# Seven block products for eight in the gate and up projections of a macaron layer

## The chip, the cores and the metric

The kernel runs on one core of a Trainium2 chip. The metric is the device time of one execution in microseconds (us). The core has a matrix engine (TensorE, PE in the profile, with its weight loads as PEld), a vector engine (DVE), a scalar engine (ACT), GpSimd (POOL) and a queue engine (SP) that issues most DMAs.

## The reference

One encoder layer on 256 tokens of width 2048, all in float32; the feed-forward width is 5632:

```python
def swiglu(h, w_gate, w_up, w_down):
    return (jax.nn.silu(h @ w_gate) * (h @ w_up)) @ w_down

x = x + 0.5 * swiglu(rms_norm(x, ffn1_norm), ffn1_w_gate, ffn1_w_up, ffn1_w_down)
# [u | q | k | v] = rms_norm(x) @ w_in; diagonal SSM on u, stick-breaking attention on q, k, v;
# x = x + concat(rms_norm(y_ssm), rms_norm(y_sb)) @ w_out
x = x + 0.5 * swiglu(rms_norm(x, ffn2_norm), ffn2_w_gate, ffn2_w_up, ffn2_w_down)
# x = x + rms_norm((p @ w_ple_proj) * sigmoid(rms_norm(x) @ w_ple_gate))
```

The change lies in `h @ w_gate` and `h @ w_up` of both feed-forward networks.

## The kernel before

**Tiling.** Tokens stand in two row tiles of 128 (`TT` = 2, index t). The contraction over 2048 has 16 k tiles of 128 (`KD`), and they are handled in quarters of four. Columns go in blocks of 512 (`NB`), so gate and up have 11 column blocks (`NF`), index f. Each FFN runs over f: `gemm_block` for the gate's block, SiLU on ACT out of PSUM (L410), `gemm_block` for up's block, then a multiplication on DVE into `hh` (L430), which `turned` transposes (two DVE transposes, L203, and DMAs into `hT`). After the 11 blocks comes the down projection, whose left side is split from `hT` by `act`.

**Three passes.** A float32 product is made of three matmuls in a rounded format: each operand is split into a high part (a cast on ACT, L168) and the remainder (a subtraction on DVE, L171); the passes are high x high, low x high and high x low. `gemm_half` (L284, L285, L289) does this for two k tiles and both row tiles: 12 matmuls of 128x128 by 128x512. The left side (the normed tokens, tiles `nhi`/`nlo` or `hhi`/`hlo`) is split once an FFN; the weights are split as they come.

**Buffers.** A quarter of k of a column block (1 MiB) is loaded by one DMA on SP's queue into `raw` (three buffers), and split into two halves of `whi`/`wlo` (four buffers each). Four PSUM accumulators (`acc`) of 512 columns take the results. `halves("n")` has four buffers of hi and lo, `halves("h")` two. In FFN 1 the left side stands in the four n buffers, and the h buffers are used from the down projection on; in FFN 2 the left side takes both h buffers and two of the n buffers.

**Order.** The program is written in one order; a scheduler then lays out each engine's queue by simulated readiness, with the written order as priority, except where `pin` holds it. `put_off(n, fn)` calls fn after n further calls of `step()`, which stands after each half. In FFN 1, the first blocks also carry side work (`s5_prep`), which is over at f = 6.

Of the kernel before, what the change touches and what calls it, by code (L numbers as in the profile page):

```python
# [9 lines left out]
F32 = mybir.dt.float32  # L10
F32R = mybir.dt.float32r
I32 = mybir.dt.int32
AF = mybir.ActivationFunctionType
ALU = mybir.AluOpType
AX = mybir.AxisListType

P = 128
# [9 lines left out]
NB = 512  # L27
# [6 lines left out]
def layer_kernel(ctx: ExitStack, tc: tile.TileContext, a: dict, shapes: dict, out: bass.AP):  # L34
    nc = tc.nc
    _, T, D = shapes["x"]
# [7 lines left out]
    TT = T // P  # L44
    ND = D // NB
    KD = D // P
    NF = F // NB
# [6 lines left out]
    wp = ctx.enter_context(tc.tile_pool(name="wts", bufs=4))  # L54
    actp = ctx.enter_context(tc.tile_pool(name="act", bufs=1))
# [8 lines left out]
    def uid(s):  # L64
        count[0] += 1
        return f"{s}_{count[0]}"

    def get(pool, tag, width=1024, bufs=1):
        return pool.tile([P, width], F32, tag=tag, name=uid(tag), bufs=bufs)

    def com(tag):
        return get(comp, tag, *{"sg": (1024, 1), "h": (1024, 2), "sq": (NB, 1), "mid": (2048, 1)}[tag])

    def phase(name):
        return tc.tile_pool(name=name, bufs=1, reuse_waits="tile")
# [4 lines left out]
    def acc(s="acc"):  # L80
        return accp.tile([P, NB], F32, tag="acc", name=uid(s))

    def small(n=8):
        return smp.tile([P, 8], F32, tag="sm", name=uid("sm"))[:, :n]
# [11 lines left out]
    def start(g):  # L96
        beside.append(g)
        return g

    def step():  # L100
        for g in list(beside):
            if next(g, beside) is beside:
                beside.remove(g)

    def finish(g):
        for _ in g:
            pass

    def put_off(steps, fn, *args):


        def g():
            for _ in range(steps):
                yield
            fn(*args)

        return start(g())

    def pin(ins):
        return tc.keep_in_program_order(ins)  # L120
# [44 lines left out]
    def split(hi, lo, src, scale=None, pinned=False):  # L165

        if scale is None:
            copy = nc.scalar.copy(hi, src)  # L168
            if pinned:
                pin(copy)  # L170
            nc.vector.tensor_tensor(out=lo, in0=src, in1=hi.bitcast(F32), op=ALU.subtract)  # L171
        else:
            split_each(hi.unsqueeze(1), lo.unsqueeze(1), src.unsqueeze(1), [scale])
# [96 lines left out]
    def weight_halves(w, k0, nk, n0, own=None):  # L270

        raw = wp.tile([P, 4, NB], F32, tag="raw", name=uid("raw"), bufs=3)
        src = w[k0 * P : (k0 + nk) * P, n0 : n0 + NB].rearrange("(j p) n -> p j n", p=P)
        nc.sync.dma_start(raw[:, :nk, :], src)
        return weight_split(raw, nk, own)

    def gemm_half(ps, half, ts, start, stop, cols=slice(0, NB)):

        (ahi, alo), (h, hi, lo) = half
        for j in range(2):  # L280
            for t in ts:
                lh = ahi[:, 2 * h + j, t * P : (t + 1) * P]
                ll = alo[:, 2 * h + j, t * P : (t + 1) * P]
                nc.tensor.matmul(ps[t], lhsT=lh, rhs=hi[:, j, cols], start=start and j == 0, stop=False)  # L284
                nc.tensor.matmul(ps[t], lhsT=ll, rhs=hi[:, j, cols], start=False, stop=False)  # L285
        for j in range(2):
            for t in ts:
                lh = ahi[:, 2 * h + j, t * P : (t + 1) * P]
                nc.tensor.matmul(ps[t], lhsT=lh, rhs=lo[:, j, cols], start=False, stop=stop and j == 1)  # L289

    def gemm_block(act, w, n0, nkt, first=()):

        ps = [acc(), acc()]
        for k0 in range(0, nkt, 4):
            part = act(k0 // 4)
            quarter = first[k0 // 4] if k0 // 4 < len(first) else weight_halves(w, k0, min(4, nkt - k0), n0)
            for half in list(quarter):
                k = k0 + 2 * half[0]
                gemm_half(ps, (part, half), range(TT), k == 0, k + 2 == nkt)
                if first and half[0] == 0 and k0 + 4 < nkt:  # L300
                    act(k0 // 4 + 1)
                step()
        return ps
# [75 lines left out]
    def ffn(i, xn, nxt, bg=None):  # L379
        wg, wu, wd = (a[f"ffn{i}_w_{s}"][0] for s in ("gate", "up", "down"))  # L380
        hT = []
        pools = ExitStack()
        early = 6 if bg else NF
        hp = pools.enter_context(phase(f"h{i}"))
        side = ExitStack()
        prep = bg(side) if bg else None
        mids = {}

        def turned(hp, f, hh):
            pair, n_pair = f // 2, min(2, NF - f // 2 * 2) * 4  # L390
            if f % 2 == 0:
                mids[pair] = com("mid")[:, : 128 * TT * n_pair].rearrange(
                    "p (q t b f) -> p q t b f", q=4, t=TT, b=32
                )
            for t in range(TT):
                turn_blocks(mids[pair], hh[:, t * NB : (t + 1) * NB], t, f % 2 * 4, 4)
            if f % 2 or f == NF - 1:
                hf = get(hp, f"hT{pair}", T * n_pair)
                turn_quarters(hf.rearrange("p (t s f) -> p t s f", t=TT, f=n_pair), mids[pair], 8)
                hT.append(hf.rearrange("p (s f) -> p f s", f=n_pair))  # L400

        for f in range(NF):
            if prep and f == min(early, NF - 1):
                finish(prep)
                side.close()
                prep = None
                hp = pools.enter_context(phase(f"h{i}b"))
            def gate():
                for t in range(TT):
                    nc.scalar.activation(sg[:, t * NB : (t + 1) * NB], pg[t], AF.Silu, scale=xn.rs(t))  # L410

            first = ()
            if f == 0 and bg:
                warm_up(10)
                first = first_quarters(wg, xn)
            pg = gemm_block(xn, wg, f * NB, KD, first)
            sg = com("sg")
            if f == 0 and bg:
                for n in range(ND):
                    put_off(n, load_x, n)  # L420
                    put_off(n + 2, xn.squares, n)
                put_off(6, gate)
            else:
                gate()
            pu = gemm_block(xn, wu, f * NB, KD)
            if prep and f == 0:
                start(prep)
            hh = com("h")
            for t in range(TT):
                nc.vector.scalar_tensor_tensor(  # L430
                    out=hh[:, t * NB : (t + 1) * NB], in0=pu[t], scalar=xn.rs(t),
                    in1=sg[:, t * NB : (t + 1) * NB], op0=ALU.mult, op1=ALU.mult,
                )
            put_off(2, turned, hp, f, hh)

        def act(k):
            hi, lo = halves("h")
            split(hi, lo, hT[k // 2][:, k % 2 * 4 : k % 2 * 4 + 4, :])
            return hi, lo

        for n in range(ND):
            ps = gemm_block(act, wd, n * NB, F // P)
            for t in range(TT):
                nc.vector.scalar_tensor_tensor(
                    out=xt[t][n], in0=ps[t], scalar=0.5, in1=xt[t][n], op0=ALU.mult, op1=ALU.add
                )
            put_off(2, nxt.block, n)
        pools.close()
# [575 lines left out]
    q0, k0, v0 = SW, SW + NH * DH, SW + 2 * NH * DH  # L1024
    mix, s5p, atp = ExitStack(), ExitStack(), ExitStack()
    mixp = mix.enter_context(phase("mix"))
    pool = s5p.enter_context(phase("s5"))
# [10 lines left out]
    pool = atp.enter_context(phase("attn"))  # L1038
# [7 lines left out]
    for n in range(2):  # L1046
        ps = gemm_block(nm, w_in, v0 + n * NB, KD)
# [6 lines left out]
    for n, side in ((0, 0), (1, 0), (0, 1), (1, 1), (2, 0), (2, 1), (3, 0), (3, 1)):  # L1054
        y, r = ((yss, rss), (ysb, rsb))[side]
        ps = gemm_block(lambda k: y[k], w_out[side * SW : (side + 1) * SW, :], n * NB, SW // P)
        for t in range(TT):
            nc.vector.scalar_tensor_tensor(
                out=xt[t][n], in0=ps[t], scalar=r[0][:, t : t + 1], in1=xt[t][n], op0=ALU.mult, op1=ALU.add
# [30 lines left out]
    for n in range(ND - 1):  # L1090
        ps = gemm_block(npl, a["w_ple_gate"][0], n * NB, KD)
        gate = com("sg"), com("h")
        for t in range(TT):
            sigmoid(gate[0], t, ps[t])
        ps = gemm_block(lambda k: pT, a["w_ple_proj"][0], n * NB, PD // P)
        for t in range(TT):
            ple(n, t, gate, ps[t])
    n = ND - 1
    gate = com("sg"), com("h")
# [8 lines left out]
    t = 0  # L1108
    sigmoid(gate[0], t, next(gates))
    ple(n, t, gate, next(projs))  # L1110
    s = small(1)
    nc.vector.tensor_reduce(out=s, in_=ss[t], axis=AX.X, op=ALU.add)
    r = rsqrt_mean(s, D, 1)
# [4 lines left out]
    t = 1  # L1118
# [3 lines left out]
    sums, part, ms, root, r, tmp = (small(ND if i == 0 else 1) for i in range(6))  # L1122
    last = small(1)
    nc.vector.tensor_copy(sums[:, : ND - 1], ss[t][:, : ND - 1])
    cols = [slice(t * NB + c * W, t * NB + (c + 1) * W) for c in range(2)]
# [10 lines left out]
    def scaled(c):  # L1136
# [15 lines left out]
        both, lhsT=diag, rhs=es[by_pe][:, t * NB : (t + 1) * NB], start=False, stop=True, skip_group_check=True  # L1152
# [75 lines left out]
```

## Time and profile before

| what | value |
|---|---|
| runs, median of 3 (lowest, highest) | 1901.69 us (1900.64, 1903.12) |
| profiled execution, first to last instruction | 1898.3 us |
| TensorE busy | 1888.4 us, 9142 matmuls |
| DVE busy | 1299.6 us |
| ACT busy | 1105.7 us |
| POOL busy | 30.6 us |
| moved by DMA | 402.55 MB, 212 GB/s mean |

The profile is of one execution. Busy times are sums over the instructions of an engine; matmuls are pipelined, so that their durations (0.39 us each) overlap and the distance between the starts of two is the better measure. A group's row has the line, the engine, the operation, what it writes and reads with its shape, the count, then busy time and mean ns, then the idle time of the engine just before it and who ended that. Rows of waits give total us, times and the longest. Windows give for each engine the busy us in the stretch.

### The profile page before, as it was taken

The numbers are of one execution on the slowest core, as the hardware profiler recorded it, in microseconds if no ns is written. First come the engines' busy times: TensorE is split into PE (matmuls) and PEld (weight loads), VectorE is DVE, ScalarE is ACT, GpSimd is POOL, SyncE is SP. The second block draws the span as 40 slices with busy tenths as digits, with TensorE's granted clock in tenths as the row PEclk, the third lists the DMA queues.
The fourth block names the chain that finished last, engine by engine and source line by source line (L and its number), as shares of the span: only waits on it lengthen the run. The fifth ranks groups of instructions, "written<-read, shape, count | busy, mean of one in ns | idle before, by whom it ended". The sixth has DMA issues, their size and how long they took to land.

```text
span 1898.3 us, 23928 instructions
## 1 busy us (share of the span) xinstructions
PE 1888.4 (99%) x9142; PEld 1563.8 (82%) x9142; DVE 1299.6 (68%) x1604; ACT 1105.7 (58%) x1217; POOL 30.6 (2%) x48
## 2 busy tenths in 40 slices
PE   9999999999999999999999999999999999999998
PEld 7888888888888888888898888888888888888886
DVE  8996765555688987686567655555555568898855
ACT  7466664444578886455785544444444457888754
POOL 0000000000000000010010000000000000000000
PEclk9999999999999999999999999999999999999999
DMA  8677877666656657776545656665656665666553
GB/s 323 225 243 260 261 247 236 197 209 209 215 185 209 209 190 277 235 243 205 172 156 172 222 187 217 200 210 191 220 189 216 201 223 188 205 209 209 196 200 122
DMA packets 225714, 402.55 MB, mean 212 GB/s; under 512 B 16704, under 2 KB 46656, under 8 KB 225472
## 3 DMA queue, kind: packets, MB, share of 16 engines
q1 hardware_dynamic: 212976, 385.99, 61.2%
q10 hardware_dynamic: 12624, 15.04, 2.3%
q8 instruction: 71, 1.16, 0.3%
q14 instruction: 43, 0.35, 0.1%
HBM read 369.53 MB, written 14.68 MB: 202 GB/s over the span
## 4 chain that ended last, share of the span: by engine, by line
PE 94%; DVE 2%; ACT 1%; issue 1%; DMA 1%; SPq 0%; DVEq 0%; ACTq 0%
PE acc L284 30%; PE acc L285 30%; PE acc L289 30%; DVE hlo L171 1%; ACT hhi L168 1%; DVE wlo L171 1%; DVE nlo L180 1%; PE aux L715 0%; PE acc L994 0%; PE acc L989 0%; PE acc L985 0%; PE aux L634 0%; DMA raw<-in_ffn_w_gate 0%; DMA h<-in_p_turned 0%; PE aux L767 0%
## 5 line engine op out<-in xcount | busy, mean ns | idle before, releaser
L171 DVE TENSOR_TENSOR wlo<-raw,whi 128x1024 fp32r<-128x1024 f32 x666 | 810.5, 1225 | 451.5 <-ACT whi L168 446.9
L168 ACT CAST whi<-raw 128x1024 fp32r<-128x1024 f32 x666 | 697.8, 1054 | 710.1 <-PE acc L285 658.4
L284 PE MATMUL acc<-whi,nhi 128*128 128x512 f32 x1568 | 614.2, 392 | 1.2 <-ACT whi L252 0.7
L285 PE MATMUL acc<-whi,nlo 128*128 128x512 f32 x1568 | 610.6, 389 | 0.0
L289 PE MATMUL acc<-wlo,nhi 128*128 128x512 f32 x1568 | 420.7, 389 | 0.0
L285 PE MATMUL acc<-whi,hlo 128*128 128x512 f32 x1056 | 411.6, 390 | 0.7
L284 PE MATMUL acc<-whi,hhi 128*128 128x512 f32 x1056 | 411.0, 389 | 0.0
L284 PEld LDWEIGHTS acc<-whi,nhi 128*128 128x128 f32 x1568 | 294.3, 188 | 64.9 <-ACT whi L252 1.8
L289 PEld LDWEIGHTS acc<-wlo,nhi 128*128 128x128 f32 x1568 | 294.2, 188 | 61.7 <-DVE wlo L171 0.2
L285 PEld LDWEIGHTS acc<-whi,nlo 128*128 128x128 f32 x1568 | 294.4, 188 | 60.0
L289 PE MATMUL acc<-wlo,hhi 128*128 128x512 f32 x1056 | 282.2, 389 | 0.0
L285 PEld LDWEIGHTS acc<-whi,hlo 128*128 128x128 f32 x1056 | 198.2, 188 | 44.7 <-DVE hlo L171 3.3
L289 PEld LDWEIGHTS acc<-wlo,hhi 128*128 128x128 f32 x1056 | 198.2, 188 | 41.2
L284 PEld LDWEIGHTS acc<-whi,hhi 128*128 128x128 f32 x1056 | 198.2, 188 | 40.7
L171 DVE TENSOR_TENSOR hlo<-hT,hhi 128x1024 fp32r<-128x1024 f32 x88 | 188.4, 2141 | 48.7 <-ACT hhi L168 48.7
L168 ACT CAST hhi<-hT 128x1024 fp32r<-128x1024 f32 x88 | 192.2, 2185 | 1.4 <-DMA raw<-in_ffn_w_gate 1.4
L203 DVE STREAM_TRANSPOSE mid<-h 128x512 f32<-128x512 f32 x44 | 47.0, 1156 | 0.0
L430 DVE SCALAR_TENSOR_TENSOR h<-acc,sm,sg 128x512 f32<-128x512 f32 x44 | 31.0, 745 | 19.4 <-PE acc L289 19.4
L410 ACT ACTIVATE sg<-acc,sm 128x512 f32<-128x512 f32 x44 | 27.7, 681 | 0.4 <-DVE sm L196 0.3
L178 ACT ACTIVATE nhi<-h,gains 128x256 fp32r<-128x256 f32 x40 | 24.0, 662 | 0.2 <-DVE h L1010 0.2
L180 DVE SCALAR_TENSOR_TENSOR nlo<-h,gains,nhi 128x256 fp32r<-128x256 f32 x40 | 23.1, 633 | 0.6 <-ACT nhi L178 0.6
L704 POOL COPY dec<-rho 128x512 f32<-128x512 f32 x8 | 10.6, 1348 | 729.0 <-DVE rt L741 564.5
(242 smaller groups left out, 762.7 us busy)
## 6 DMA issues: line engine op xcount, KB each, us to landing
raw<-in_ffn_w_up SPq DMA_DIRECT2D x88, 1024.0 KB, 5.5
raw<-in_ffn_w_down SPq DMA_DIRECT2D x88, 1024.0 KB, 5.0
raw<-in_ffn_w_gate SPq DMA_DIRECT2D x86, 1024.0 KB, 5.1
raw<-in_w_in SPq DMA_DIRECT2D x32, 1024.0 KB, 5.5
raw<-in_w_out SPq DMA_DIRECT2D x16, 1024.0 KB, 5.2
raw<-in_w_ple_gate SPq DMA_DIRECT2D x16, 1024.0 KB, 5.0
hT<-mid SPq DMA_DIRECT2D x160, 64.0 KB, 4.8
h<-mid SPq DMA_DIRECT2D x128, 32.0 KB, 3.7
```

Source lines behind the costliest of these rows:

```text
L168: copy = nc.scalar.copy(hi, src)
L171: nc.vector.tensor_tensor(out=lo, in0=src, in1=hi.bitcast(F32), op=ALU.subtract)
L178: nc.scalar.activation(hi[:, j, :], src[:, j, :], AF.Copy, scale=scale)
L180: nc.vector.scalar_tensor_tensor(out=lo[:, j, :], in0=src[:, j, :], scalar=scale, in1=hi[:, j, :].bitcast(F32), op0=ALU.mult, op1=ALU.subt ...
L203: nc.vector.transpose(mid[:, :, t, :, k0 : k0 + nk].rearrange("p q b f -> p f q b"), src.rearrange("p (f q b) -> p f q b", f=nk, q=4),)
L284: nc.tensor.matmul(ps[t], lhsT=lh, rhs=hi[:, j, cols], start=start and j == 0, stop=False)
L285: nc.tensor.matmul(ps[t], lhsT=ll, rhs=hi[:, j, cols], start=False, stop=False)
L289: nc.tensor.matmul(ps[t], lhsT=lh, rhs=lo[:, j, cols], start=False, stop=stop and j == 1)
L410: nc.scalar.activation(sg[:, t * NB : (t + 1) * NB], pg[t], AF.Silu, scale=xn.rs(t))
L430: nc.vector.scalar_tensor_tensor(out=hh[:, t * NB : (t + 1) * NB], in0=pu[t], scalar=xn.rs(t), in1=sg[:, t * NB : (t + 1) * NB], op0=ALU.m ...
L704: nc.gpsimd.tensor_copy(dvw[:, i], rho4[:, 8 * q : 8 * q + 8].unsqueeze(2).to_broadcast([P, 8, NC]))
```

## The change

From the block after the first one (FFN 1: from f = 7, as the side work lies before; FFN 2: from f = 1) gate and up of one column block are computed together in a new function `pair`: 4 blocks in FFN 1 and 10 in FFN 2. For the first quarter of k, the product of the 2x2 block matrix A (row tiles x k halves of 256) and the 2x2 block matrix B (k halves x [gate, up]) is computed by Winograd's form of Strassen's method: seven block products with four sums of blocks of A, four sums of blocks of B and seven sums of products, in place of eight. The other three quarters of k go on as before, in `rest`, and accumulate into the same PSUM banks.

- `quarter_sums` makes the four sums of A once an FFN on DVE and splits them.
- `fetch(f + 1)` stands in the written order after the products of f. It loads the first quarter of gate and up (`dg`, `du`, 1 MiB each) and three further copies of halves (`t1`, `t2`, `t4`, 0.5 MiB each) on SP's queue. Four DMAs issued by POOL add into SBUF: up's upper half onto t1, up's lower half onto its upper half in `du`, t1 onto t2, t2 onto t4. The tiles t1, t2, t4 and `kept` take buffers of h (FFN 1) or n (FFN 2).
- `pair` runs the seven products, each with its own split of the right side (`product`, 6 matmuls), at most three splits written ahead. Four intermediate values are copied out of PSUM by ACT (o6, o1, o5, o7; o6 and o7 are the halves of `kept`). Three sums among them are put off by three steps. At the end two subtractions come before the two multiplications into `hh`.

```diff
-    def gemm_half(ps, half, ts, start, stop, cols=slice(0, NB)):
+    def gemm_half(ps, half, ts, start, stop, cols=slice(0, NB), **kw):
...
+    def product(ps, a, src, start):
+
+        (ahi, alo), hi, lo = a, *(wp.tile([P, 2, NB], F32R, tag=s, name=uid(s)) for s in ("whi", "wlo"))
+        split(hi, lo, src)
+
+        def run():
+            for j in range(2):
+                for i, l in enumerate((ahi, alo)):
+                    nc.tensor.matmul(
+                        ps, lhsT=l[:, j], rhs=hi[:, j], start=start and i + j == 0, stop=False, skip_group_check=True
+                    )
+            for j in range(2):
+                nc.tensor.matmul(ps, lhsT=ahi[:, j], rhs=lo[:, j], start=False, stop=j == 1, skip_group_check=True)
+
+        return run
+
+    def quarter_sums(pool, part):
+
+        hi, lo = part
+        full, s = (com("h").rearrange("p (j t) -> p j t", t=T), com("h").rearrange("p (i j t) -> p i j t", i=4, j=2))
+        nc.vector.tensor_tensor(out=full, in0=hi.bitcast(F32), in1=lo.bitcast(F32), op=ALU.add)
+        a11, a12, a21 = (full[:, 2 * k : 2 * k + 2, t * P : (t + 1) * P] for t, k in ((0, 0), (0, 1), (1, 0)))
+        a22 = full[:, 2:, P:]
+        for o, x, y, op in (
+            (0, a21, a22, ALU.subtract), (1, s[:, 0], a11, ALU.subtract), (2, a11, a21, ALU.subtract),
+            (3, a12, s[:, 1], ALU.add),
+        ):
+            nc.vector.tensor_tensor(out=s[:, o], in0=x, in1=y, op=op)
+        shi, slo = (pool.tile([P, 4, 2, P], F32R, name=uid(n)) for n in ("shi", "slo"))
+        split(shi, slo, s)
...
+        first_pair = (early if bg else 0) + 1
+        spare = "h" if bg else "n"
+        left, right = [], {}
+
+        def fetch(f):
+
+            dg, du = (get(hp, s, 4 * NB).rearrange("p (j n) -> p j n", j=4) for s in ("dg", "du"))
+            t1, t2, t4, kept = (
+                actp.tile([P, 1024], F32, tag=spare + s, name=uid("t"), bufs={"n": 4, "h": 2}[spare])
+                for s in ("hi", "lo", "hi", "lo")
+            )
+            t1, t2, t4 = (t.rearrange("p (j n) -> p j n", j=2) for t in (t1, t2, t4))
+            gate, up = (w[:NB, f * NB : (f + 1) * NB].rearrange("(j p) n -> p j n", p=P) for w in (wg, wu))
+            for d, b in ((t1, gate[:, :2]), (t2, up[:, 2:]), (dg, gate), (du, up), (t4, gate[:, 2:])):
+                nc.sync.dma_start(d, b)
+            b11, b21, b12, b22 = dg[:, :2], dg[:, 2:], du[:, :2], du[:, 2:]
+            right[f] = b11, b21, b22, t1, t2, b12, t4, kept
+            for d, b in ((t1, up[:, :2]), (b12, up[:, 2:]), (t2, t1), (t4, t2)):
+                nc.gpsimd.dma_start(d, b, accum_op=ALU.add)
+
+        def rest(ps, w, f, starts):
+            for k0 in range(4, KD, 4):
+                part = xn(k0 // 4)
+                for half in list(weight_halves(w, k0, 4, f * NB)):
+                    k = k0 + 2 * half[0]
+                    gemm_half(
+                        ps, (part, half), range(TT), starts if k == 4 else False, k + 2 == KD, skip_group_check=True
+                    )
+                    step()
+
+        def pair(f, prefetch):
+
+            (a11, a12, a22), (s1, s2, s3, s4) = left[0]
+            b11, b21, b22, t1, t2, t3, t4, kept = right.pop(f)
+            x, a, y = acc(), acc(), acc()
+            o6, o7 = kept[:, :NB], kept[:, NB:]
+            o1, o5 = get(hp, "o1", NB), get(hp, "o5", NB)
+            todo = [
+                (x, s2, t2, o6), (a, a11, b11, o1), (y, s1, t1, o5), (x, s3, t3, o7), (a, a12, b21, None),
+                (y, s4, b22, None), (x, a22, t4, None),
+            ]
+            runs = []
+            for i, (ps, l, r, o) in enumerate(todo):
+                while len(runs) < min(i + 3, len(todo)):
+                    n = len(runs)
+                    runs.append(product(*todo[n][:3], todo[n][3] is not None and n != 3))
+                runs[i]()
+                if o is not None:
+                    nc.scalar.copy(o, ps)
+                if i % 2 or i == 6:
+                    step()
+            if prefetch:
+                fetch(f + 1)
+
+            def sums():
+                nc.vector.tensor_tensor(out=o6, in0=o6, in1=o1, op=ALU.add)
+                nc.vector.tensor_tensor(out=o7, in0=o7, in1=o1, op=ALU.add)
+                nc.vector.tensor_tensor(out=o7, in0=o7, in1=o5, op=ALU.subtract)
+
+            put_off(3, sums)
+            rest([a, x], wg, f, ())
+            sg = com("sg")
+            nc.scalar.activation(sg[:, :NB], a, AF.Silu, scale=xn.rs(0))
+            nc.vector.tensor_tensor(out=sg[:, NB:], in0=x, in1=o1, op=ALU.add)
+            nc.scalar.activation(sg[:, NB:], sg[:, NB:], AF.Silu, scale=xn.rs(1))
+            z = acc()
+            rest([y, z], wu, f, (1,))
+            hh = com("h")
+            for ps, o in ((y, o6), (z, o7)):
+                nc.vector.tensor_tensor(out=o, in0=ps, in1=o, op=ALU.subtract)
+            for t, o in enumerate((o6, o7)):
+                sl = slice(t * NB, (t + 1) * NB)
+                nc.vector.scalar_tensor_tensor(
+                    out=hh[:, sl], in0=o, scalar=xn.rs(t), in1=sg[:, sl], op0=ALU.mult, op1=ALU.mult
+                )
+            put_off(2, turned, hp, f, hh)
+
         for f in range(NF):
...
+            if f >= first_pair:
+                pair(f, f + 1 < NF)
+                continue
+
             def gate():
...
+            if f + 1 == first_pair:
+                left.append(quarter_sums(hp, xn(0)))
+                fetch(f + 1)
             pu = gemm_block(xn, wu, f * NB, KD)
```

More of the change, by code (lines that the diff above doesn't have):

```diff
@@ L275, in weight_halves @@
         return weight_split(raw, nk, own)
-    def gemm_half(ps, half, ts, start, stop, cols=slice(0, NB)):
+    def gemm_half(ps, half, ts, start, stop, cols=slice(0, NB), **kw):
         (ahi, alo), (h, hi, lo) = half
+        starts = (ts if start else ()) if isinstance(start, bool) else start
         for j in range(2):
@@ L283, in gemm_half @@
                 ll = alo[:, 2 * h + j, t * P : (t + 1) * P]
-                nc.tensor.matmul(ps[t], lhsT=lh, rhs=hi[:, j, cols], start=start and j == 0, stop=False)
-                nc.tensor.matmul(ps[t], lhsT=ll, rhs=hi[:, j, cols], start=False, stop=False)
+                nc.tensor.matmul(ps[t], lhsT=lh, rhs=hi[:, j, cols], start=t in starts and j == 0, stop=False, **kw)
+                nc.tensor.matmul(ps[t], lhsT=ll, rhs=hi[:, j, cols], start=False, stop=False, **kw)
         for j in range(2):
@@ L288, in gemm_half @@
                 lh = ahi[:, 2 * h + j, t * P : (t + 1) * P]
-                nc.tensor.matmul(ps[t], lhsT=lh, rhs=lo[:, j, cols], start=False, stop=stop and j == 1)
+                nc.tensor.matmul(ps[t], lhsT=lh, rhs=lo[:, j, cols], start=False, stop=stop and j == 1, **kw)
+    def product(ps, a, src, start):
[23 more added lines that the diff above has]
+        split(shi, slo, s)
+        quarters = [
+            tuple(u[:, 2 * k : 2 * k + 2, t * P : (t + 1) * P] for u in part) for t, k in ((0, 0), (0, 1), (1, 1))
+        ]
+        return quarters, [(shi[:, i], slo[:, i]) for i in range(4)]
     def gemm_block(act, w, n0, nkt, first=()):
@@ new lines, in rest @@
+        def rest(ps, w, f, starts):
[16 more added lines that the diff above has]
+                (y, s4, b22, None), (x, a22, t4, None),
+            ]
+            runs = []
[31 more added lines that the diff above has]
+            put_off(2, turned, hp, f, hh)
```

## Prediction

> **What bounds the kernel now.** I read the page first (spans, busy shares, the chain that ended last), then TensorE's own waits, then one block of FFN 2 as a window and as a timeline, at last the DMA view of the same window.
>
> ```profile
> span 1898.3 us, 23928 instructions
> PE 1888.4 (99%) x9142; PEld 1563.8 (82%) x9142; DVE 1299.6 (68%) x1604; ACT 1105.7 (58%) x1217; POOL 30.6 (2%) x48
> ...
> PE 94%; DVE 2%; ACT 1%; issue 1%; DMA 1%; SPq 0%; DVEq 0%; ACTq 0%
> ```
>
> The chain is 94% matmuls, and the waits of TensorE, longest first, are nothing beside them:
>
> ```profile
> PE aux L1151 <- ACT diag L1150: 2.8, 1, 2.8
> PE aux L227 <- POOL ones L126: 1.1, 1, 1.1
> ```
>
> So the time is a count of matmuls times their pitch, and a removed matmul is worth its pitch as long as nothing else comes late. One gate/up block of FFN 2 as a window (from one DVE epilogue to the next), then a stretch at the kernel's start in which the DMA engines are full:
>
> ```profile
> core 0: us, PE busy (x) PEld busy (x) DVE busy (x) ACT busy (x) POOL busy (x), PEclk, DMA share, GB/s
> 1200.35:1243.87 43.52, 43.52 (x193) 36.04 (x192) 22.81 (x21) 18.04 (x19) 0.00 (x0) 1.00 0.59 195
> ...
> 4.00:34.00 30.00, 28.84 (x127) 23.05 (x126) 27.07 (x77) 21.75 (x38) 0.00 (x0) 1.00 1.05 390
> ```
>
> A block is 16 k tiles x 2 row tiles x 3 passes x 2 (gate and up) = 192 matmuls in 43.52 us: pitch 0.2267 us at full granted clock. DVE is busy 22.81 us of it, ACT 18.04, the DMA engines 59%. The second row says what the DMA engines can carry: 390 GB/s for 30 us on end.
>
> **The saving.** A pair's first quarter of k was 8 block products of 6 matmuls, 48; it becomes 7 of 6, 42. All stay 128x512 and the other three quarters are unchanged (144). 6 x 0.2267 = 1.36 us a pair, a block shrinks to 42.16 us, and 14 pairs (4 in FFN 1, f = 7 to 10; 10 in FFN 2, f = 1 to 10) give **-19.04 us**.
>
> The page "TensorE: Matmul & The Clock Gate" of the Trainium skill, section "Back-to-back issue gap", gives about 131 ns a matmul for streams of 512 columns. By that the 84 matmuls were worth 11.0 us and the time 1894.2 instead of the forecast below. The trace disagrees (226.7 ns), and the trace decides.
>
> **Work added on DVE and ACT, per pair.** The rows that price it:
>
> ```profile
> L171 DVE TENSOR_TENSOR wlo<-raw,whi 128x1024 fp32r<-128x1024 f32 x666 | 810.5, 1225 | 451.5 <-ACT whi L168 446.9 <-DMA hT<-mid 1.5
> L168 ACT CAST whi<-raw 128x1024 fp32r<-128x1024 f32 x666 | 697.8, 1054 | 710.1 <-PE acc L285 658.4 <-DMA raw<-in_ffn_w_gate 6.9 <-DVE rot L550 5.4
> L171 DVE TENSOR_TENSOR hlo<-hT,hhi 128x1024 fp32r<-128x1024 f32 x88 | 188.4, 2141 | 48.7 <-ACT hhi L168 48.7
> L430 DVE SCALAR_TENSOR_TENSOR h<-acc,sm,sg 128x512 f32<-128x512 f32 x44 | 31.0, 745 | 19.4 <-PE acc L289 19.4
> L813 ACT ACTIVATE sg<-acc,sm 128x512 f32<-128x512 f32 x8 | 5.0, 680 | 0.0
> L754 DVE TENSOR_TENSOR rt<-rt,rt 128x504 f32<-128x504 f32 x8 | 5.0, 663 | 0.0
> L1081 DVE TENSOR_TENSOR h<-acc,sg 128x512 f32<-128x512 f32 x7 | 4.6, 687 | 9.6 <-PE acc L289 9.6
> L548 DVE TENSOR_TENSOR cm<-rot,s5s 128x256 f32<-128x256 f32 x16 | 5.9, 417 | 0.0
> ```
>
> Seven splits replace four: 3 x 1.225 on DVE, 3 x 1.054 on ACT. New on ACT: four copies of 512 columns out of PSUM, 4 x 0.68. New on DVE: two subtractions at the end and one addition for the second gate row from PSUM (3 x 0.687), three sums in SBUF (3 x 0.663). Together DVE +7.7 (30.5 of 42.2 us) and ACT +5.9 (23.9): no engine becomes the bound over a pair. The once-per-FFN sums of the left side are DVE 1.225 + 4 x 0.417 + 1.225 = 4.1 us and ACT 1.05, in a block where DVE has 20.7 us idle: nothing. Without that cover they would cost 5 us an FFN.
>
> **Where it is tight: the first 11 us of a pair.** A product feeds TensorE for 1.36 us where a half fed it 2.72, so splits are wanted twice as fast there, while the epilogue of the last pair is longer. Timeline of a block's end, DVE, ACT and TensorE:
>
> ```profile
> 1198.03 1.23 DVE L171 TENSOR_TENSOR wlo<-raw,whi 128x1024 fp32r<-128x1024 f32 x1 [1.50 <-ACT whi L168]
> 1200.35 1.41 DVE L430 SCALAR_TENSOR_TENSOR h<-acc,sm,sg 128x512 f32<-128x512 f32 x2 [1.09 <-PE acc L289]
> 1201.67 1.21 DVE L171 TENSOR_TENSOR wlo<-raw,whi 128x1024 fp32r<-128x1024 f32 x1
> 1202.80 2.14 DVE L203 STREAM_TRANSPOSE mid<-h 128x512 f32<-128x512 f32 x2
> 1204.77 1.23 DVE L171 TENSOR_TENSOR wlo<-raw,whi 128x1024 fp32r<-128x1024 f32 x1
> ...
> 1199.66 1.05 ACT L168 CAST whi<-raw 128x1024 fp32r<-128x1024 f32 x1 [1.67 <-PE acc L285]
> ...
> 1199.24 0.39 PE L285 MATMUL acc<-whi,nlo 128*128 128x512 f32 x1
> 1199.47 1.07 PE L289 MATMUL acc<-wlo,nhi 128*128 128x512 f32 x4
> 1200.37 0.39 PE L284 MATMUL acc<-whi,hhi 128*128 128x512 f32 x1
> ```
>
> The cast at 1199.66 starts as the last half's whi passes end (1199.24 + 0.39): the four whi buffers are all in use, so the splits of the next three halves are done when the block ends, and DVE goes straight to the epilogue. I count from T = 1200.37, the next block's first matmul.
>
> DVE after the change: epilogue of two subtractions and two products, 2.8 us (the two of today take 1.41), then the splits of products 4 to 7 about 1.2 us apart (done at T+4.0, 5.2, 6.4, 7.6), the two transposes, put off by two steps and so traced behind the last product's split (9.6), then the first half of the rest (10.8). TensorE wants the wlo of product n at (6(n-1)+4) x 0.2267: T+5.0, 6.35, 7.7, 9.1 for 4 to 7, and of that first half at (42+8) x 0.2267 = T+11.3. Every split is 0.5 to 1.5 us early.
>
> ACT: casts wait for a whi buffer, four matmuls into each product, and are 1.05 long; between them stand the copies. The first (o6) writes the tile `kept`, two buffers of which one holds the split-off t2; so it waits for the last pair's epilogue to have read it, T+2.8. With a cast ahead of it, it ends at T+4.0; product 4 adds to the same PSUM bank from 18 x 0.2267 = T+4.08. Products 5, 6 and 7 need their copies at T+5.4, 6.8 and 8.2, and by the same listing they are there 0.5 to 1.2 us earlier. So the wait on o6 decides: 0 when it goes first, about 1 us (one cast more in front of it) at worst. TensorE's queue would hold the remaining products behind it. I take 0.2 us a pair, near the clear end: **+2.8 us** (0 to 14).
>
> **The end of FFN 1.** There t1, t2, t4 and `kept` live in the hhi/hlo buffers which the down projection uses for its first two activations; now these are split long ahead:
>
> ```profile
> 499.98 1.41 DVE L430 SCALAR_TENSOR_TENSOR h<-acc,sm,sg 128x512 f32<-128x512 f32 x2 [1.09 <-PE acc L289]
> 501.30 1.22 DVE L171 TENSOR_TENSOR wlo<-raw,whi 128x1024 fp32r<-128x1024 f32 x1
> 502.43 2.00 DVE L203 STREAM_TRANSPOSE mid<-h 128x512 f32<-128x512 f32 x2
> 504.29 1.19 DVE L171 TENSOR_TENSOR wlo<-raw,whi 128x1024 fp32r<-128x1024 f32 x1
> 505.82 1.23 DVE L171 TENSOR_TENSOR wlo<-raw,whi 128x1024 fp32r<-128x1024 f32 x1 [0.34 <-ACT whi L168]
> 507.89 2.14 DVE L171 TENSOR_TENSOR hlo<-hT,hhi 128x1024 fp32r<-128x1024 f32 x1 [0.85 <-ACT hhi L168]
> ```
>
> The hlo at 507.89 is the third; the second becomes possible only when the epilogue has released `kept` (T+2.8), takes 2.14 and is wanted at 24 x 0.2267 = T+5.4. If a wlo and the transposes go first it is some 3 us late. Once: I take **+0.7 us** (0 to 3). FFN 2 uses the n buffers, which its down projection does not touch; there only the epilogue's extra 1.4 us meets idle DVE.
>
> **DMAs.** Issues and waits of the raw loads in the gate/up blocks of FFN 2, and the window's traffic:
>
> ```profile
> SPq L274 <- DVE wlo L171: 301.0, 67, 5.9
> ...
> raw<-in_ffn_w_up SPq DMA_DIRECT2D x4, 1024.0 KB, 5.0
> raw<-in_ffn_w_gate SPq DMA_DIRECT2D x4, 1024.0 KB, 5.1
> ...
> DMA packets 4252, 8.47 MB, mean 195 GB/s; under 512 B 128, under 2 KB 128, under 8 KB 4250
> ```
>
> A block moves 8.47 MB. Two loads of 1 MiB go, five (3.5 MiB) come: +1.57 MB. Four adds move 0.5 MiB each: 2.10 MB if a byte counts once. 12.1 MB in 42.16 us is 288 GB/s, 74% of the 390 of the full stretch. No row shows an adding DMA, nor one issued by POOL. From below: 0, as the next pair's operands are wanted some 30 us after they can be fetched (raw loads land in 5; the chain is one load and three adds). From above: the engines hold 390 x 42.16 = 16.4 MB a pair, so an add may cost 3 times a plain copy of its bytes before the DMAs set the pace. Beyond that each further unit costs 2.10 MB / 390 = 5.4 us a pair. I take 0, since the nearest rows, plain copies, leave a factor of three.
>
> The page "DMA: Bandwidth & Descriptors" of the Trainium skill, section "Rules for kernel authors", says that an accumulating DMA reads its destination and writes it later. No run here shows it. If that doubles the bytes, 14.2 MB in 42.16 us is 338 GB/s, 87%, and the sum stays.
>
> On SP's queue the five loads stand among the raw loads. SP waits for wlo splits today (301 us in 67 waits), so it has time; the loads wait for product splits up to about T+7.6, and a raw load behind them is late by that plus their 3.67 MB / 390 = 9.4 us. The raws of the gate's rest have their three buffers free before T, and the fourth is not due for issue before its buffer is split at about T+12; it is wanted at (42 + 6 x 12) x 0.2267 = T+25.8, less 2.3 for its split. Landing within 11 us of its issue does; cost 0. POOL's four adds wait for loads and for each other, with nothing else behind them (POOL is idle in the window).
>
> **Sum.** -19.04 + 2.8 + 0.7 = -15.5 us on a profiled span of 1898.3, so 1882.8. The median of the runs is 1901.69, 3.4 above that span and its runs lie within 2.5; carried over: **1886.2 us**.
>
> **Rivals.**
> 1. *The product stretch starves* (DVE order or the wait on `kept`). Speaks for it: margins of 0.1 to 0.5 us on two waits, a transposing pair of 2.0 us that, placed one split earlier, makes product 7 0.5 late. Against: DVE still has 11.7 us idle per pair. Price 0.7 to 1.7 us a pair: from 1892 to 1906, in the middle 14 x 1.2 - 19 = -2.2, 1899.5. At 1.36 nothing is left.
> 2. *The other side: the adds fill the DMA engines.* From 3.3 times a copy's cost (43.52 x 390 = 17.0 MB, less 10.04, over 2.10) the pair is longer than before; at 4 times it is 18.4 MB / 390 = 47.3 us, +3.8 x 14 = +53: 1955. For it: nothing in the trace bounds an add. Against: the factor of three. The same page, section "Queues, rings and completion order", has each DMA engine serve its queues in turn, by which raw loads would slow down beside the adds; no row here shows two long queues together.
> 3. *Raw loads wait behind the fetch on SP.* The fourth raw's slack is 23.5 - 12 - 5.1 = 6.4 us; behind all five loads it is 9.4 - 6.4 = 3.0 us late, which less the saving is +1.64 x 14 = +23: 1925. Against: the order above, in which the fetch falls into a stretch without raw splits.
>
> **How the numbers follow.** Forecast 0.62 (its own range 1882 to 1892: the saving whole, or another 0.5 us a pair lost), rival 1 0.16, rival 2 0.12, rival 3 0.10. What can be told from no change is 0.2%, 3.8 us: 1897.9 to 1905.5. Faster is the forecast and over half of rival 1, 0.71; same 0.05 from the rest of it; slower rivals 2, 3 and rival 1's tail, 0.24. The range from 1881.5 (all of the saving, and the runs' spread) to 1906 takes in the forecast and rival 1, 0.78.
>
> **What would show it.** Matmuls 9142 less 84. Block windows of 42.2 to 42.5 us; 43.5 means rival 1. TensorE's waits naming an ACT copy of a product (o6) or a wlo, a few tenths each, show the tight places; a wait for raw or for t2/t4 shows rivals 2 or 3, with the DMA share near 1 and landings of raw far over 5.1 us. DVE near 30 us a pair. The prediction is wrong if the pitch is not kept across the change of operands at each product, if an add costs over three copies, or if the scheduler puts fetch loads in front of raws that are due.

## The result, and the profile after

| | median of runs | ratio to before, 95% interval |
|---|---|---|
| before | 1902.13 us (8 runs) | |
| changed | 1907.14 us (8 runs, 1904.80 to 1912.36) | 1.0029 [1.0017, 1.0042] |

The forecast was 1886.2 us. The kernel became slower by 0.3%, where a gain was forecast, and its time lies above the range. The profiled execution took 1904.92 us with a span of 1903.1, 4.8 us above the span of before. Its page:

```profile
span 1903.1 us, 24345 instructions
PE 1878.0 (99%) x9058; PEld 1548.3 (81%) x9058; DVE 1393.9 (73%) x1742; ACT 1168.5 (61%) x1317; POOL 92.1 (5%) x104
...
q1 hardware_dynamic: 224400, 408.01, 63.7%
q0 software_dynamic: 11648, 29.36, 8.3%
...
PE 81%; DMA 9%; DVE 5%; ACT 2%; issue 2%; SPq 1%; DVEq 0%; ACTq 0%
...
raw<-in_ffn_w_down SPq DMA_DIRECT2D x88, 1024.0 KB, 5.1
raw<-in_ffn_w_up SPq DMA_DIRECT2D x74, 1024.0 KB, 9.1
```

The 84 matmuls are gone (9058). But the chain that ended last now runs through DMAs for 9%, where it had 1%, and a raw load of up lands 9.1 us after its issue (the median of the whole run; 13.6 among the pairs of FFN 2, from 1100 to 1500 us), one of down still 5.1. TensorE waits for casts that wait for those loads; the longest waits of its weight loads:

```profile
PEld acc L285 <- ACT whi L168: 20.8, 14, 3.1
```

Windows from one pair's epilogue to the next show where. FFN 2, f = 1 to 5, then f = 9 and 10:

```profile
1112.74:1155.14 42.40, 42.40 (x187) 34.92 (x186) 28.10 (x27) 22.50 (x26) 4.27 (x4) 1.00 0.93 285
1155.14:1202.02 46.88, 44.24 (x187) 35.93 (x186) 28.86 (x29) 22.21 (x26) 4.24 (x4) 0.96 0.90 258
1202.02:1244.87 42.85, 42.71 (x187) 34.84 (x186) 29.07 (x31) 22.25 (x26) 4.27 (x4) 1.00 0.99 307
1244.87:1291.48 46.61, 43.11 (x188) 34.82 (x187) 28.87 (x30) 22.28 (x26) 4.25 (x4) 1.00 0.90 259
1291.48:1334.08 42.60, 42.60 (x187) 34.80 (x186) 29.06 (x30) 22.23 (x26) 4.25 (x4) 1.00 0.99 307
...
1467.91:1510.91 43.00, 42.65 (x187) 34.78 (x186) 29.07 (x31) 22.12 (x26) 4.24 (x4) 1.00 0.98 306
1510.91:1553.31 42.40, 42.40 (x187) 34.93 (x186) 33.50 (x32) 26.84 (x28) 0.00 (x0) 1.00 0.62 193
```

(Columns: stretch and length, then busy us of TensorE, its weight loads, DVE, ACT, POOL, the granted clock, DMA share, GB/s.) An undisturbed pair takes 42.40 us, 1.12 less than the 43.52 of before; 14 of these are -15.7. But the pairs in which the transposed pieces of h are on SP's queue (even f, since the pieces of two blocks go out together) take 45.0 to 46.9: the five of them that also fetch (f = 8 in FFN 1; 2, 4, 6 and 8 in FFN 2) lose 18.1 us over 42.40, all other pairs 1.0. The remaining +1.4 came before and between the pairs. Two controls stand in the trace itself: odd pairs fetch and have no pieces, and f = 10 has pieces and fetches nothing; neither is much longer than 42.40 (at most 43.00).

The mechanism is in SP's queue (SPq) of pair f = 4, and in the chain over the same stretch:

```profile
1249.78 0.37 SPq L452 DMA_DIRECT2D dg<-in_ffn_w_gate  x1
1250.91 0.37 SPq L452 DMA_DIRECT2D du<-in_ffn_w_up  x1
1252.05 0.37 SPq L452 DMA_DIRECT2D t<-in_ffn_w_gate  x1
1256.43 0.37 SPq L274 DMA_DIRECT2D raw<-in_ffn_w_up  x1
1256.85 2.54 SPq L216 DMA_DIRECT2D hT<-mid  x4
1259.49 0.54 SPq L274 DMA_DIRECT2D raw<-in_ffn_w_up  x1
1260.32 18.06 SPq L216 DMA_DIRECT2D hT<-mid  x8
1278.48 0.53 SPq L274 DMA_DIRECT2D raw<-in_ffn_w_up  x1
...
1259.49 18.29 DMA raw<-in_ffn_w_up
1277.88 1.05 ACT whi L168
1284.73 1.04 ACT whi L168
```

The second raw load of up goes out at 1259.49 and lands 18.29 us later, at 1277.78. Eight pieces behind it occupy the queue for 18.06 us, and the third raw load goes out only at 1278.48, although its buffer had been free since 1262.7, when DVE finished the last split that reads it. SP's waits in this pair put a name to it:

```profile
SPq L216 <- DMA raw<-in_ffn_w_up: 10.4, 2, 5.8
```

A piece reads `mid` and writes `hT`; it needs nothing of a raw load. Counted in the listing, the piece that starts at 1268.93 is the eighth DMA behind the raw load of 1256.43, which had just landed, and the one at 1277.80 the eighth behind that of 1259.49: a DMA on this queue goes out no earlier than the one eight places ahead has landed. The whole trace bears this out: of 769 DMAs on SP's queue none goes out before the one eight ahead has landed, while 93 go out before the one seven ahead has; in the kernel before it is 0 of 727, and 45. In the trace's records SP's DMAs signal eight semaphores, and the piece at 1268.93 waits for the one which that raw load signals and which it signals itself. So the limit is one of the program as it was built; whether the chip's queue has one of its own no run shows, and no experiment changed the number. So a late load passes its delay on to whatever stands behind it.

### The profile page after: what moved, and what is told of

The parts are those of the page before. It is cut to its first block, busy times and chain, and to the rows that moved or that the text cites. A ratio compares the mean times of both kernels' runs of the same rounds, so it can differ in the third digit from the quotient of the medians.

```text
span 1903.1 us, 24345 instructions
## 1 busy us (share of the span) xinstructions
PE 1878.0 (99%) x9058; PEld 1548.3 (81%) x9058; DVE 1393.9 (73%) x1742; ACT 1168.5 (61%) x1317; POOL 92.1 (5%) x104
## 3 DMA queue, kind: packets, MB, share of 16 engines
q0 software_dynamic: 11648, 29.36, 8.3%
## 4 chain that ended last, share of the span: by engine, by line
PE 81%; DMA 9%; DVE 5%; ACT 2%; issue 2%; SPq 1%; DVEq 0%; ACTq 0%
PE acc L285 24%; PE acc L286 24%; PE acc L290 23%; DMA raw<-in_ffn_w_up 7%; PE acc L300 5%; PE acc L304 2%; DVE wlo L171 2%; DMA raw<-in_ffn_w_down 1%; DVE hlo L171 1%; ACT hhi L168 1%; SPq L216 1%; DVE nlo L180 1%; ACT whi L168 1%; PE aux L835 0%; PE acc L1114 0%
## 5 line engine op out<-in xcount | busy, mean ns | idle before, releaser
L168 ACT CAST whi<-raw 128x1024 fp32r<-128x1024 f32 x610 | 634.7, 1053 | 593.7 <-PE acc L286 347.4
L171 DVE TENSOR_TENSOR wlo<-raw,whi 128x1024 fp32r<-128x1024 f32 x610 | 735.5, 1225 | 354.6 <-ACT whi L168 329.0
L285 PE MATMUL acc<-whi,nhi 128*128 128x512 f32 x1504 | 591.9, 394 | 15.7 <-ACT whi L168 14.7
L286 PE MATMUL acc<-whi,hlo 128*128 128x512 f32 x896 | 349.5, 390 | 0.8 <-DVE hlo L171 0.3
L285 PE MATMUL acc<-whi,hhi 128*128 128x512 f32 x896 | 348.8, 389 | 0.0
L290 PE MATMUL acc<-wlo,hhi 128*128 128x512 f32 x896 | 239.5, 389 | 0.0
L286 PEld LDWEIGHTS acc<-whi,hlo 128*128 128x128 f32 x896 | 168.2, 188 | 39.0 <-DVE hlo L171 3.8
L171 DVE TENSOR_TENSOR wlo<-t,whi 128x1024 fp32r<-128x1024 f32 x42 | 51.2, 1220 | 8.7 <-ACT whi L168 8.6
L168 ACT CAST whi<-t 128x1024 fp32r<-128x1024 f32 x42 | 44.2, 1053 | 13.3 <-PE acc L286 13.3
L300 PE MATMUL acc<-whi,shi 128*128 128x512 f32 x112 | 44.5, 397 | 0.0
L300 PE MATMUL acc<-whi,slo 128*128 128x512 f32 x112 | 44.1, 394 | 0.0
```

The costliest lines, as they stand in the source:

```text
L285: nc.tensor.matmul(ps[t], lhsT=lh, rhs=hi[:, j, cols], start=t in starts and j == 0, stop=False, **kw)
L300: nc.tensor.matmul(ps, lhsT=l[:, j], rhs=hi[:, j], start=start and i + j == 0, stop=False, skip_group_check=True)
```

## The experiments

All runs were timed beside runs of the kernel before on the same chip (median 1902 to 1904). Pair lengths below are of FFN 2.

**Leaving out the adds.**

```diff
-            for d, b in ((t1, up[:, :2]), (b12, up[:, 2:]), (t2, t1), (t4, t2)):
-                nc.gpsimd.dma_start(d, b, accum_op=ALU.add)
```

> The four adds of each pair are left out (their operands stay the plain loads), all loads stay. Theory A, the adding DMAs fill the DMA engines so that the raw loads of up land late: every pair takes 42.3 to 42.5 us, also those with transposed pieces on the queue (45.0 to 46.9 now), and the time is about 1887 (1905 - 18). Theory B, the extra 1.5 MiB of loads in a burst are enough: pairs with pieces stay at 44 or more, 1895 to 1903. Theory C, the order on SP's queue (raw loads behind pieces that wait): pairs with pieces stay at 45 or more, above 1900.

Measured: 1885.06 us, ratio 0.9907 [0.9890, 0.9924]. All ten pairs take 42.40. The loads remain, 261 GB/s in a pair with pieces, and here too eight pieces hold the queue for 8.51 us, but the raw loads of up land in 6.7, and TensorE waits for none of them:

```profile
1194.45:1236.85 42.40, 42.40 (x187) 34.91 (x186) 29.51 (x30) 22.82 (x26) 0.00 (x0) 1.00 0.76 261
...
1252.80 8.51 SPq L216 DMA_DIRECT2D hT<-mid  x8
1261.40 0.53 SPq L274 DMA_DIRECT2D raw<-in_ffn_w_up  x1
```

Theory B (the extra loads are enough) is out, and theory C alone as well: the adds are necessary.

**The same DMAs as copies.**

```diff
-                nc.gpsimd.dma_start(d, b, accum_op=ALU.add)
+                nc.gpsimd.dma_start(d, b)
```

> The same four DMAs from POOL with the same sources, targets and bytes, but copying where they added. If the adding makes them slow (0.5 MiB in 8 to 10 us, 186 GB/s on their queue), copies land in 4 to 6 us and the time is near that without them, 1887 to 1892. If it is the bytes or the second queue, they behave as the adds do: 1903 to 1908.

Measured: 1886.19 us, 0.9917 [0.9898, 0.9936]. POOL's queue moved the same bytes:

```profile
q0 software_dynamic: 8064, 29.36, 4.1%
```

29.36 MB took 8.3% of 16 engines' time with adding and 4.1% without: an add costs 2.0 times a copy. The copies landed in 5.6 to 7.5 us, in part above the 4 to 6 expected, and the raw loads of up in 10.6, between the 6.7 without them and the 13.6 with adds. The bytes on a second queue make the loads later but cost about 1 us; the other 21 are the adding.

**Pieces on POOL's queue.**

```diff
-                    nc.sync.dma_start(
+                    (queue or nc.sync).dma_start(   # queue = nc.gpsimd from the first pair on
```

> The transposed pieces of h (16 small DMAs for each two blocks) go to POOL's queue from the first pair on; the adds stay. Theory C: raw loads are issued as their buffers come free, the slow pairs fall from 45-47 to about 42.5, 1888 to 1892. Theory A: raw loads of up still land 12 us and more after issue; pairs stay at 44 to 46, 1898 to 1907.

Measured: 1890.34 us, 0.9935 [0.9915, 0.9954]. The adds are all there and raw loads of up land in 14.6 us, later than in the changed kernel; pairs with pieces take 42.9 to 44.5. So A's number for the landings came true and C's for the time: late loads cost little here, where the next load is not held back too.

**Pieces left out.** POOL fills their targets with zeros instead.

```diff
+                if f >= first_pair:
+                    nc.gpsimd.memset(hf, 0.0)
+                else:
                     turn_quarters(...)
```

> From the first pair on the pieces are left out altogether (POOL fills their targets with zeros); adds and all loads stay. If pieces are the second half of the trouble, all pairs are 42.3 to 42.9 us and the time is 1885 to 1889. If the adds alone make the raw loads late, pairs of 44 and more remain, 1893 and above.

Measured: 1890.44 us, 0.9936 [0.9919, 0.9952], as with the pieces on the other queue, though raw loads of up land in 15.4 us. A pair that would have pieces, then one that would not:

```profile
1152.56:1195.24 42.68, 42.68 (x187) 34.84 (x186) 29.06 (x29) 22.19 (x26) 4.24 (x4) 1.00 0.93 283
1195.24:1237.82 42.58, 42.58 (x187) 34.85 (x186) 29.07 (x30) 22.20 (x26) 4.27 (x4) 1.00 0.94 284
```

The adds alone cost the 5 us between this run and the one without adds; the pieces alone cost nothing there; together they cost 22 (1907 against 1885). In the run with the pieces on POOL's queue their bytes move all the same, so the pieces' traffic is not the matter, their place on SP's queue is. The time came out 1.4 above what was expected, and pairs reach 43.1 us instead of 42.9.

**Pieces earlier, and pieces held later.**

```diff
-                turn_quarters(..., mids[pair], 8)
+                turn_quarters(..., mids[pair], 0 if f >= first_pair else 8)
```

> The transposed pieces stay on SP's queue but are called right after the transposes instead of eight steps later, so they are not between the raw loads of up. Theory C (a raw load waits on SP behind pieces that wait for an earlier load to land): the raw of up are issued as their buffers come free, 1888 to 1895. If the bytes and the slow adds delay the raw loads anyway: pairs with pieces stay at 45 and more, 1902 to 1908.

Measured: 1947.23 us, 1.0224 [1.0209, 1.0239], the worst of all. In a pair with pieces:

```profile
1271.74 2.51 SPq L216 DMA_DIRECT2D hT<-mid  x4
...
1274.97 12.44 SPq L216 DMA_DIRECT2D hT<-mid  x12
1287.51 2.81 SPq L274 DMA_DIRECT2D raw<-in_ffn_w_up  x3
```

I had expected a gain from taking them out from between the loads. Now all 16 stand ahead of all three, hold the queue for 15.7 us, and all three go out after 1287. The other way round:

```diff
+                    if hold:
+                        pin(piece)          # behind the DMA written before it
...
-                turn_quarters(..., mids[pair], 8)
+                turn_quarters(..., mids[pair], 11 if first_pair <= f < NF - 1 else 8, first_pair <= f < NF - 1)
```

> Adds, loads and pieces all stay, and the pieces stay on SP's queue, but each is held behind the DMA written before it and they are called three steps later, so they stand behind the last raw load of up instead of before it. If the trouble is a raw load standing on SP behind a piece that waits until the load eight places ahead has landed, the time falls to that without pieces or with the pieces on POOL's queue: 1888 to 1893, pairs of 42.3 to 44.3. If the pieces' traffic or SP's time to issue them (0.6 us each) is the trouble, pairs with pieces stay at 45 to 47: 1902 to 1908.

Measured: 1908.38 us, 1.0032 [1.0019, 1.0045]: no gain, and the expectation missed. The loads of up now go out before the pieces, and the delay moves on:

```profile
1260.34 6.67 SPq L276 DMA_DIRECT2D raw<-in_ffn_w_up  x3
1267.07 21.97 SPq L216 DMA_DIRECT2D hT<-mid  x16
1289.13 1.11 SPq L276 DMA_DIRECT2D raw<-in_ffn_w_gate  x2
```

The pieces take 22 us behind the loads of up, and the next pair's gate loads (T = 1291.7) go out at 1289 instead of some 10 us before T. The pairs with pieces now take 42.4 to 44.1 us; the pairs that follow them take 43.6 to 48.7. In the one from 1291.7 to 1338.3 the late gate loads meet the fetch, the loads of up land 15.8 to 19.4 us after issue, and TensorE waits until 1320.29 for up's first raw load. That pair loses 4 us with no piece on its queue. Both runs move the same pieces on the same queue: whichever raw load stands behind them goes out late. These two runs cannot tell the pieces' waiting from SP's plain time to issue them (0.6 us each, 10 of the 22). Other rows do: of the 18.06 us in the changed kernel 10.4 are waits for raw loads, and without the adds the same 16 issues cost no pair anything.

**Spreading the fetch.** Each of the five loads is pinned behind a raw load, one every step or two, and the adds follow.

> All loads and adds of the change stay, but the five loads are held behind one raw load each and the adds follow them, so that the fetch is spread over the pair's rest. If the pair lacks DMA capacity on average (an add costs twice a copy: 10.0 MB / 0.39 + 4.2 MB / 0.39 = 36.5 us of 42.4), nothing lacks and the time is 1886 to 1891: the burst was the fault. If adds cost more beside other queues, so that the engines are full over the whole pair, it stays at 1898 to 1907.

Measured: 1908.05 us, 1.0028 [1.0013, 1.0043]: the burst is not the fault by itself. In a pair with pieces the queue holds again, now behind a load of the fetch (dg lands after 13.8 us):

```profile
1264.59 14.02 SPq L216 DMA_DIRECT2D hT<-mid  x8
1278.70 0.53 SPq L454 DMA_DIRECT2D t<-in_ffn_w_gate  x1
1279.34 0.44 SPq L274 DMA_DIRECT2D raw<-in_ffn_w_up  x1
```

The expectation's other branch (the engines lack time over the whole pair) isn't shown by this either: with the same adds, the runs without pieces on SP are 18 us faster.

**The fetch on POOL's queue.** The five loads by `nc.gpsimd.dma_start`.

> Adds and pieces stay as in the change; the five loads of the fetch (3.5 MiB) go to POOL's queue, so that SP's queue holds only raw loads and pieces. If raw loads are late because they stand behind the fetch in SP's one queue (rival 3), they land in 5 to 8 us, the pieces behind them go out at once and the time is 1886 to 1892. If they are late because fetch and adds take the DMA engines' time whatever the queue, raw loads of up still land 11 us and more after issue, the pieces hold the next raw back, and the time stays at 1900 to 1908.

Measured: 1922.15 us, 1.0091 [1.0070, 1.0111]: neither branch of the expectation, and above both. With nothing but raw loads and pieces on SP, raw loads of up still land in 9.2 us, those of gate in 11.0. But POOL's queue became a bottleneck of its own: POOL stood up to 10 us before a DMA with no wait that shows, each time until 0.3 to 0.7 us after the DMA one or two places ahead on its queue had landed. TensorE waits for product copies as well. Whether the queue or the engines' time delays the loads stays open.

**The sums without DMAs: on DVE, on POOL.**

```diff
-            for d, b in ((t1, gate[:, :2]), (t2, up[:, 2:]), (dg, gate), (du, up), (t4, gate[:, 2:])):
+            for d, b in ((dg, gate), (du, up)):
...
-            for d, b in ((t1, up[:, :2]), (b12, up[:, 2:]), (t2, t1), (t4, t2)):
-                nc.gpsimd.dma_start(d, b, accum_op=ALU.add)
+            def add(o, x, y):
+                nc.vector.tensor_tensor(out=o, in0=x, in1=y, op=ALU.add)
+
+            for i, oxy in enumerate(((t1, b11, b12), (t2, t1, b22), (b12, b12, b22), (t4, t2, b21))):
+                put_off((3 if f == first_pair else 5) + i, add, *oxy)
```

> No adds and no extra loads: dg and du are loaded once (2 MiB, as many bytes as before the change), and the four sums are four DVE additions of 1024 columns (4 x 1.22 us a pair) put off into the second half of the gate's rest. Theories A and B: DMA share falls back to about 0.6, all pairs 42.4, 1886 to 1888. If DVE (33.9 of 42.4 us busy then) delays a split, TensorE waits for wlo and the time lies above 1892.

Measured: 1888.70 us (1885.35 to 1892.47), 0.9932 [0.9910, 0.9954]. This beats both kernels, though the median lies 0.7 above the 1886 to 1888 expected. In the profiled execution, the fastest of the four (1885.35), all pairs take 42.40 with 8 MiB of loads, and DVE is busy 33.7 of it; what made the others longer it can't show:

```profile
1152.29:1194.69 42.40, 42.40 (x187) 34.93 (x186) 33.68 (x33) 22.73 (x26) 0.00 (x0) 1.00 0.69 223
```

The same on POOL (`nc.gpsimd.tensor_tensor`):

> As e4 (2 MiB loaded, no adds by DMA), but the four sums of 1024 columns run on POOL (994 ns for 256 columns in the profile of before, so some 3.9 us each, 16 us a pair, where POOL is idle). If only the DMAs mattered: 42.4 us a pair, 1885 to 1889 as with the sums on DVE. If POOL's reads slow DVE's subtractions, wlo comes late in the product stretch: DVE's 1.22 us splits grow, above 1890.

Measured: 1895.99 us (1889.83 to 1900.32), 0.9960 [0.9944, 0.9977]: a gain, but a part of it is lost. The profiled execution is the slowest (1900.32). POOL's four additions, then DVE in the same stretch:

```profile
1172.63 3.18 POOL L457 TENSOR_TENSOR t<-dg,du 128x1024 f32<-128x1024 f32 x1 [32.02 <-DMA du<-in_ffn_w_up]
1175.89 2.74 POOL L457 TENSOR_TENSOR t<-t,du 128x1024 f32<-128x1024 f32 x1
1178.57 2.87 POOL L457 TENSOR_TENSOR du<-du 128x1024 f32<-128x1024 f32 x1
1181.41 3.38 POOL L457 TENSOR_TENSOR t<-t,dg 128x1024 f32<-128x1024 f32 x1
...
1173.42 2.94 DVE L497 TENSOR_TENSOR t<-t,o 128x512 f32<-128x512 f32 x1
1176.29 2.89 DVE L498 TENSOR_TENSOR t<-t,o 128x512 f32<-128x512 f32 x1
1179.10 3.42 DVE L171 TENSOR_TENSOR wlo<-raw,whi 128x1024 fp32r<-128x1024 f32 x1
```

A DVE sum of 512 columns takes 2.9 us instead of the 0.69 with the sums on DVE, a subtraction of 1024 takes 3.4 instead of 1.22. Beside an addition on POOL, a DVE instruction with two operands in SBUF lasts about as long as that addition, as if the two engines took turns by whole instructions; these times suggest it, no run separates it. TensorE's weight loads wait for wlo 17.5 us in all.

## Why the prediction was wrong, point by point

**The saving** held in kind: 84 matmuls at 0.2267 us would be 19.04. But the pitch is not kept. The 42 matmuls of the products take 9.76 us (first start 1244.89, first of the rest 1254.65), 0.2324 each, +0.24 us a pair or 3.4 in all. That gives 42.16 + 0.24 = 42.40, seen in every undisturbed pair. The prediction itself had named this among the three things that would make it wrong; in the sum, the 2.8 us taken for another reason cover most of it.

**The tight first 11 us** did not bite. DVE ran as listed (from T: epilogue, splits of products 4 to 7, transposes), here in pair f = 4:

```profile
1244.87 1.29 DVE L507 TENSOR_TENSOR t<-acc,t 128x512 f32<-128x512 f32 x2 [1.09 <-PE acc L290]
1246.07 1.41 DVE L510 SCALAR_TENSOR_TENSOR h<-t,sm,sg 128x512 f32<-128x512 f32 x2
1247.39 1.22 DVE L171 TENSOR_TENSOR wlo<-du,whi 128x1024 fp32r<-128x1024 f32 x1
...
1250.80 1.22 DVE L171 TENSOR_TENSOR wlo<-t,whi 128x1024 fp32r<-128x1024 f32 x1
1251.94 2.29 DVE L203 STREAM_TRANSPOSE mid<-h 128x512 f32<-128x512 f32 x2
```

The term of 2.8 us for the wait on `kept` was the wrong reason with nearly the right size, by luck: there was no such wait, and the pitch cost 3.4. Rival 1 is out. The end of FFN 1 cost at most the 0.4 us by which the stretch between the two FFNs' epilogues (499.01 to 1112.74) is longer than before, inside the 0 to 3; the tail after the last pair is 349.8 us long in both traces.

**The DMA step failed**: it put at 0 what cost 18.1 us in five pairs, in two places. The first is its sentence "Landing within 11 us of its issue does; cost 0": the raw loads of up in pair f = 4 landed 12.5 and 18.3 us after issue. The step worked out the need of one load, the fourth raw, which is up's first. That one, late by its own bound, still did not stop TensorE. TensorE's weight loads wait 2.82 us for the fifth and 1.52 us for the sixth, which the step does not look at. An add was priced safely inside the factor of three, and it is (2.0). But I set the bytes against the whole pair's 42 us, and that average says nothing of a queue whose loads have 6.4 us of slack each: pair f = 1 lost nothing at a DMA share of 0.93. The Trainium skill's statement that an accumulating DMA reads its destination and writes it later ("DMA: Bandwidth & Descriptors", "Rules for kernel authors") fits the measured factor of 2.0; I had weighed it against the average as well.

The second place is an omission: the 16 pieces on SP's queue appear nowhere in the step. In the profile of before SP's waits showed them, waiting for the transposes, and also a raw load waiting for another raw load to land. These are the two rows right below the one that the prediction quotes (FFN 2, 1110 to 1500 us):

```profile
SPq L216 <- DVE mid L203: 6.7, 4, 1.7
SPq L274 <- DMA raw<-in_ffn_w_up: 3.1, 4, 1.4
```

Without the pieces the late loads cost 5 us instead of 22. The span came out 20.3 us above the forecast one: the 18.1 in these five pairs, and the 1.0 and 1.4 found above, while the 3.4 of pitch stand where the forecast had 3.5.

Rival 3, which had 0.10, named a part of this: up's first raw load does stand behind all five loads of the fetch. But in the run without adds it stands there too and costs nothing, so that order alone is not the cause; the adds make the loads late, and the pieces pass it on to the next load.

Rival 2 (engines full over the pair, threshold 3.3) did not occur, though the DMA share of 0.9 to 1.0 comes close; its outcome, slower, came by late raw loads as in rival 3, and at a fifth of that rival's forecast price of +23.

## What to carry to other kernels

A transfer that is off the critical path is priced by the queue it stands in, not by the share of bandwidth: list what stands behind it, when each of these is wanted, and what a late landing holds back. A cheaper matrix algorithm that pays with operand sums should take them from an engine with idle time in that stretch, here DVE, which in the changed kernel is idle some 13 us of a pair (29.1 of 42.4 busy), before the DMA engines. And an idle engine is not always free to use: POOL was idle, but its additions made DVE's sums beside them some four times as long (2.9 us for 0.69).

## What the runs showed of the hardware that was not expected

- An adding DMA takes 2.0 times the DMA engines' time of a copy of the same bytes (8.3% against 4.1% for 29.36 MB), and 0.5 MiB lands in 8 to 10 us.
- As this program is built, a DMA on SP's queue goes out no earlier than the one eight places ahead has landed (0 of 769 did), whether or not their data are related.
- Additions on POOL slow DVE's two-operand instructions in SBUF from 0.69 to 2.9 us. The Trainium skill states such a contention ("SBUF — State Buffer", "Who interferes with whom"): an instruction of DVE with two SBUF inputs against a POOL instruction that reads SBUF. The trace agrees.
- In the changed kernel, TensorE came back from a wait of 3.06 us with a granted clock of 0.57 in the mean of 4 us, which added some 1.6 us to the stall (the pair of 46.88); after one of 2.82 us the clock stayed at 1.00. The length of the wait alone does not decide it: with the fetch spread, the clock was 0.63 from 1463 to 1467 us, after a wait of 2.4 us that ended at 1461.9, and 1.00 in the 4 us after one of 2.9 that ended at 412.0. Here are the two waits in the changed kernel, and the 4 us around the end of the first:

```profile
1189.49 0.29 PEld L285 LDWEIGHTS acc<-whi,nhi 128*128 128x128 f32 x1 [3.06 <-ACT whi L168]
1278.97 0.19 PEld L285 LDWEIGHTS acc<-whi,nhi 128*128 128x128 f32 x1 [2.82 <-ACT whi L168]
...
1189.00:1193.00 4.00, 3.51 (x9) 2.79 (x10) 2.96 (x3) 2.69 (x4) 0.00 (x0) 0.57 0.75 200
```

- Streams of six matmuls with changing left operands and PSUM banks ran at 0.2324 us each, those of twelve at 0.2267; why was not tested.
